# Expert slots by rank, an earlier routing order and moved operands in a two-block transformer kernel

## The chip, the cores and the metric

The kernel runs on one core of one Trainium2 chip. The metric is the device time of one execution in microseconds (us). Five engines run their own instruction streams: TensorE (PE; its weight loads are listed as PEld), VectorE (DVE), ScalarE (ACT), GpSimd (POOL) and SyncE (SP), which here issues nearly all DMAs.

## The reference

256 tokens of width 1024 pass through two blocks. The first has two layers, each a mixer (attention with pooling in layer 0, gating with convolution in layer 1) and a mixture of experts (MoE). The second has two layers of attention branches and an MLP. The change is mostly in the MoE of the first block:

```python
g_prob = softmax(t @ rg_w + rg_b); g_p, g_idx = top_k(g_prob, 1)            # 4 groups
e_sel = e_logits[group g_idx]                                               # 4 experts of the group
top_p, top_i = top_k(softmax(e_sel), 2); top_p = top_p / sum(top_p)
weights = g_p * top_p; expert_id = g_idx * 4 + top_i                        # 2 of 16 experts per token
for wg, wu, wd, cw in experts:
    acc = acc + ((silu(t @ wg) * (t @ wu)) @ wd) * cw[:, None]
```

So 512 assignments of tokens to 16 experts are computed in each layer, and how many tokens an expert has is known only on the chip.

## The kernel before

**The MoE.** `moe` computes router logits (lg) and from them the chosen experts (selb); products with triangular and all-ones matrices (rank, L490 to L494) give each token its place among the tokens of its expert (rk) and each expert its count (cn). One-hot matrices (oh; weighted ow) are built from the places by `slots`; `gather` multiplies the normed tokens, as high and low parts whi and wlo, with oh into the slots of a group of experts (gps, L543, evicted as xg or ug); `up` makes the gate and up products (gu, L566), `turn` transposes and weights (htp, L580), `down` makes the down product (yp, L600) and scatters back to tokens (y, L609) with ow transposed. A slot group has 256 columns: four experts of 64 slots (CAP), and `prepare(q)` builds group q.

**The steps.** STEPS has seven steps. Experts 0 to 3 are fixed and fill steps one and two, so their weights are loaded ahead (`chunk`). The other twelve are sorted by their counts: `key`, `more`, `perm`, `order`, and as integers `ints` (L642 to L658). SyncE reads these (TENSOR_LOAD, L725) before it issues the load of an expert's weights (`dyn`, L730). Step five holds four experts of 32 slots as four column tiles of TensorE, the others two experts of 64 slots as two tiles of 64 columns. Up, gather and down of neighbouring steps are interleaved on TensorE.

**Overflow.** `more_blocks` counts what doesn't fit. In the last round the engines read `over` and `rest` (L725) and branch (L788): if any expert has more than its slots, `overflow` runs gather, up, turn and down once more for the two largest, whose weights were kept (step LAST), and under L791 and L793 further blocks for other experts.

**Order and queues.** Each engine runs its stream in the order of the built program, which a scheduler makes from the code; `keep_in_program_order` pins an instruction. Between router and gather TensorE has products for the conditioning (mps<-w,cpad, L382), which `cond` spreads over the program. Weights come in 1 MB chunks through rings of 13 slots; SyncE issues them in order and waits when no slot is free.

**Products in three parts.** `mm3` (L168 to L170) makes each fp32 product of 256 columns as three: weights whi with moving high part, whi with low part, wlo with high part. `split` (L140, L141) makes whi and wlo from a chunk on ScalarE and VectorE. `tm` (L201 to L203) does the same with 512 columns. The MLP up products are fm<-oTh, its down products d<-hidh; the attention projections are fm<-acth, those of the mixers fm<-ah.

**Start.** `warm(22)` issues bf16 products on zeros at the start of the program; the first mixer's tm products follow the first conditioning round (`cond.finish()`).

Of the kernel before, what the change touches and what calls it, by code (L numbers as in the profile page):

```python
# [49 lines left out]
NC1 = _lay(C1T, [("stri", 128), ("cos2d", 128), ("sin2d", 128), ("slot", 64), ("first", 4), ("rank", 12), ("gap", 38), ("less", 16)])  # L50
# [9 lines left out]
STEPS = ((0, 1), (2, 3), (4, 5), (6, 7), (8, 9, 10, 11), (12, 13), (14, 15))  # L60
PART = ((0, 0), (0, 1), (1, 0), (1, 1), (2, 0), (3, 0), (3, 1))
LAST = 6
RANKS = (2, 3, 4, 5, 8, 9, 10, 11, 6, 7, 1, 0)
# [4 lines left out]
def build(tc, I, O):  # L68
# [3 lines left out]
    with es:  # L72
# [3 lines left out]
        psum = es.enter_context(tc.tile_pool(name="psum", bufs=1, space=PSUM))  # L76

# [32 lines left out]
        ring_b = b1.enter_context(tc.tile_pool(name="ring_b", bufs=7))  # L110
        pb = c1.tile([128, NPB], F32, name="pb")
# [7 lines left out]
        epst = const.tile([128, 16], F32, name="epst")[:, 0:1]  # L119
# [308 lines left out]
        def moe(layer, norm, rc, work, blocks):  # L428
# [29 lines left out]
            def b4(x):  # L458
                return x.to_broadcast([128, 2, 4, 4])

            red(em, le, ALU.max)
            red(gm, gl, ALU.max)
            V.tensor_tensor(e2, le, b4(em), op=ALU.subtract)
            A.activation(e2, e2, AF.Exp)
            V.tensor_tensor(ge, gl, bc(gm, 4), op=ALU.subtract)
            A.activation(ge, ge, AF.Exp)
            V.tensor_tensor(oe, gl, bc(gm, 4), op=ALU.is_equal)
            V.tensor_tensor(oe, oe, FG, op=ALU.mult)
            red(es_, e2, ALU.add)
            red(om, oe, ALU.max)  # L470
            V.reciprocal(es_, es_)
            V.tensor_tensor(og, oe, bc(om, 4), op=ALU.is_equal)
            V.tensor_tensor(pr, e2, b4(es_), op=ALU.mult)
            red(gs, ge, ALU.add)
            V.reciprocal(gp, gs)

            p8 = pr.rearrange("p b g j -> p (b g) j")
            other, own = (p8.unsqueeze(i).to_broadcast([128, 8, 4, 4]) for i in (2, 3))
            V.tensor_tensor(eq, other, own, op=ALU.is_equal)
            V.tensor_tensor(gt, other, own, op=ALU.is_gt)  # L480
            V.tensor_tensor(eq, eq, C("less").rearrange("p (i j) -> p i j", i=4).unsqueeze(1)
                            .to_broadcast([128, 8, 4, 4]), op=ALU.mult)
            V.tensor_tensor(gt, gt, eq, op=ALU.add)
# [13 lines left out]
            V.tensor_tensor(sel, pr.rearrange("p b g j -> p b (g j)"), selb, op=ALU.mult)  # L497
            red(om, sel, ALU.add)
            V.reciprocal(om, om)
            V.tensor_tensor(om, om, gp, op=ALU.mult)  # L500
            V.tensor_tensor(cw, sel, bc(om, 16), op=ALU.mult)

# [5 lines left out]

            rk = t(16, "rk")
# [4 lines left out]
            def slots(n, ranks, weights, cap=CAP):  # L514

                shape = [128, n, CAP]
                oh = small.tile([128, 2, n, CAP], F32R, name="oh", tag=f"oh{n}", bufs=2 if n == 4 else 1)
                ow = small.tile([128, 2 * n * CAP], F32, name="ow", tag=f"ow{n}", bufs=2 if n == 4 else 1)
                ow = ow[:, 0:2 * n * cap].rearrange("p (b n s) -> p b n s", b=2, n=n)
                for b in range(2):  # L520
                    V.tensor_tensor(oh[:, b], C("slot").unsqueeze(1).to_broadcast(shape),
                                    ranks[:, b].unsqueeze(2).to_broadcast(shape), op=ALU.is_equal)
                    V.tensor_tensor(ow[:, b], oh[:, b, :, 0:cap].bitcast(F32),
                                    weights[:, b].unsqueeze(2).to_broadcast([128, n, cap]), op=ALU.mult)
                return oh, ow
# [3 lines left out]
            def gather(oh, n):  # L529

                w = n * CAP
                flip[0] ^= n == 4
                if flip[0] or n < 4:
                    xg = small.tile([128, NK, w], F32, name="xg", tag="xg")
                else:
                    xg = c1.tile([128, NK, w], F32, name="ug", tag="ug")
                per = 512 // w
                for q in range(NK // per):
                    gp_ = (ops if q % 2 else acc)("gps")
                    for m, (part, b) in enumerate((p_, b_) for p_ in (ah, al) for b_ in range(2)):  # L540
                        for i in range(per):
                            k = per * q + i
                            T.matmul(gp_[:, w * i:w * i + w], part[b][:, 128 * k:128 * k + 128],  # L543
                                     oh[:, b].rearrange("p e s -> p (e s)"),
                                     start=(m == 0 and i == 0), stop=(m == 3), skip_group_check=True)
# [10 lines left out]
            def up(x_, s0, gus, between=lambda: None, n=2):  # L556

                each = 128 // n
                gu = acc("gu")
                for h in range(2):  # L560
                    if h:
                        between()
                    w = [gus(h, e) for e in range(n)]
                    for k in range(4):
                        for e in range(n):
                            T.matmul(gu[each * e:each * e + each, :],  # L566
                                     x_[:, 4 * h + k, s0 + CAP * e:s0 + CAP * e + each],
                                     w[e][:, 512 * k:512 * k + 512],
                                     start=(h == 0 and k == 0), stop=(h == 1 and k == 3),
                                     tile_position=(0, each * e))  # L570
# [20 lines left out]
            def down(turned, dns, first, last, n=2):  # L591
                ht, back, cws = turned
                each = 128 // n
                wd = [dns(e) for e in range(n)]
                yg = pair([128, D], "yg", small, bufs=2)
                for q in range(2):
                    yp = (ops if q else acc)("yp")
                    for k in range(2):
                        for e in range(n):
                            T.matmul(yp[each * e:each * e + each, :],  # L600
                                     ht[:, 128 * k + each * e:128 * k + each * e + each],
                                     wd[e][:, 1024 * k + 512 * q:1024 * k + 512 * q + 512],
                                     start=(k == 0), stop=(k == 1), tile_position=(0, each * e))
# [11 lines left out]
            g2 = const.tile([128, NK], F32, name=f"g2_{layer}")  # L615
# [5 lines left out]

            def prepare(q):
                oh, ow = slots(4, (rkp if q else rk)[:, :, 4 * q:4 * q + 4], (cwp if q else cw)[:, :, 4 * q:4 * q + 4],
                               CAP // 2 if q == 2 else CAP)
                if q == 0:
# [7 lines left out]
                quarter[q] = gather(oh, 4), ow  # L633
# [4 lines left out]

            iota = C("slot")[:, 0:16]
            order, key, more_ = (small.tile([128, 16], F32, name=n, tag=n) for n in ("order", "key", "more"))  # L640
            few = small.tile([128, 24], F32, name="few", tag="few")[:, 0:16]
            V.scalar_tensor_tensor(key, cn, 16.0, iota, op0=ALU.mult, op1=ALU.add)  # L642
            in2 = small.tile([128, 12, 16], F32, name="in2", tag="in2")
            perm = small.tile([128, 12, 16], F32, name="perm", tag="perm")
            G.memset(perm, 0.0)
            G.memset(more_, 0.0)
            shape = [128, 12, 12]
            V.tensor_tensor(in2[:, :, 0:12], key[:, 4:16].unsqueeze(1).to_broadcast(shape),
                            key[:, 4:16].unsqueeze(2).to_broadcast(shape), op=ALU.is_gt)
            V.tensor_reduce(more_[:, 4:16], in2[:, :, 0:12], axis=AX.X, op=ALU.add)  # L650
            V.tensor_tensor(perm[:, :, 4:16], more_[:, 4:16].unsqueeze(1).to_broadcast(shape),
                            C("rank").unsqueeze(2).to_broadcast(shape), op=ALU.is_equal)
            shape = [128, 12, 16]
            V.tensor_tensor(in2, perm, iota.unsqueeze(1).to_broadcast(shape), op=ALU.mult)
            V.tensor_reduce(order[:, 4:16], in2, axis=AX.X, op=ALU.add)
            ints = small.tile([128, 16], I32, name="ints", tag="ints")
            intr = small.tile([128, 10], I32, name="intr", tag="intr")
            V.tensor_copy(ints[:, 4:16], order[:, 4:16])  # L658

            rkp, cwp = t(16, "rkp"), t(16, "cwp")  # L660
            for dst_, src_ in ((rkp, rk), (cwp, cw)):
                for b in range(2):
                    V.tensor_tensor(in2, perm, src_[:, b].unsqueeze(1).to_broadcast(shape), op=ALU.mult)
                    V.tensor_reduce(dst_[:, b, 4:16], in2, axis=AX.X, op=ALU.add)
# [3 lines left out]
            def more_blocks():  # L668
# [3 lines left out]
                ov, ov2, cnt, last = (small.tile([128, 16], F32, name=n, tag=n) for n in ("ov", "ov2", "cnt", "last2"))  # L672
                rest = small.tile([128, 2], F32, name="rest", tag="rest")
# [3 lines left out]
                V.scalar_tensor_tensor(key, few, CAP / 2, cn, op0=ALU.mult, op1=ALU.add)  # L677
# [1196 lines left out]
```

## Time and profile before

| what | value |
|---|---|
| median of 3 runs | 1494.14 us (1490.57 to 1494.27) |
| the profiled execution | 1494.22 us, span 1492.5 us |
| mean granted TensorE clock | 0.985 |
| busy: PE, DVE, ACT, POOL | 1453.1, 851.7, 654.1, 27.3 us |
| HBM read | 322 MB, 216 GB/s over the span |

How to read it: the first block runs to about 600 us (the MoE of layer 0 from about 172 to 334, of layer 1 from about 458 to 594), the second block after it in two similar halves. Idle time of an engine matters only where TensorE waits for that engine. A clock of 1.00 in a stretch is 2.4 GHz, 0.5 is 1.2 GHz. Matmuls are pipelined, so the time from the start of one to the start of the next is what a product costs, not its own listed duration.

### The profile page before, as it was taken

The page shows a single profiled execution, that of the slowest core. Times are in us where ns is not written, and L with a number is a line of the kernel's source. Part 1 is how long each engine was busy: PE and PEld are TensorE (multiplying, and loading weights), DVE is VectorE, ACT ScalarE, POOL GpSimd, SP SyncE. Part 2 cuts the span into 40 slices and gives each one's busy share as a digit, 9 for nine tenths or more (in the row PEclk, how much of TensorE's full clock was granted, in tenths as well). Part 3 has the DMA queues.
Part 4 walks back from the last instruction along what each step waited for, and adds up shares of the span by engine and source line. Part 5 has one row for each costly group of instructions (what it writes and reads, how often), then busy time and mean ns, then how long its engine had stood idle before and what let it go on. Part 6 is the DMA issues. An engine that isn't in the chain of part 4 may idle for free.

```text
span 1492.5 us, 25477 instructions
## 1 busy us (share of the span) xinstructions
PE 1453.1 (97%) x10370; PEld 1168.0 (78%) x10372; DVE 851.7 (57%) x1666; ACT 654.1 (44%) x1108; POOL 27.3 (2%) x63
## 2 busy tenths in 40 slices
PE   8999899989999998999999999999999999999998
PEld 3756644446985443798789999999898799999998
DVE  2765452126637222758776765556759767755554
ACT  2544311124433111565664554444565654644443
POOL 0000000000000000010000000000100000000000
PEclk9999999999999999999999999999999999999999
DMA  9964799949484986644125555553443234555540
GB/s 394 400 283 171 296 372 366 398 167 374 173 335 191 404 360 238 211 158 171 58 90 193 191 205 183 185 197 143 155 167 144 69 131 170 188 208 198 177 162 29
DMA packets 47006, 324.85 MB, mean 218 GB/s; under 512 B 5601, under 2 KB 5985, under 8 KB 8481
## 3 DMA queue, kind: packets, MB, share of 16 engines
q1 hardware_dynamic: 45360, 320.12, 56.3%
q8 instruction: 86, 1.41, 0.4%
q10 hardware_dynamic: 1296, 1.55, 0.3%
q0 software_dynamic: 224, 1.46, 0.3%
q14 instruction: 40, 0.32, 0.1%
HBM read 322.06 MB, written 1.05 MB: 216 GB/s over the span
## 4 chain that ended last, share of the span: by engine, by line
PE 57%; DVE 2%; ACT 1%; issue 0%; DVEq 0%; ACTq 0%
PE fm L169 10%; PE fm L170 10%; PE fm L168 10%; PE d L169 4%; PE d L168 4%; PE d L170 4%; PE sp L1504 1%; PE tm L201 1%; PE tm L202 1%; PE tm L203 1%; PE lf L169 1%; PE lf L170 1%; PE lf L168 1%; PE po L1493 1%; PE ptp L1487 1%; DVE wlo L141 1%
## 5 line engine op out<-in xcount | busy, mean ns | idle before, releaser
L141 DVE TENSOR_TENSOR wlo<-w,whi 128x1024 fp32r<-128x1024 f32 (+1 forms) x314 | 378.4, 1208 | 254.1 <-ACT whi L140 252.9
L140 ACT CAST whi<-w 128x1024 fp32r<-128x1024 f32 (+1 forms) x314 | 324.3, 1035 | 388.2 <-PE fm L169 234.7
L168 PE MATMUL fm<-acth,whi 128*128 128x256 f32 x592 | 169.4, 286 | 0.0
L169 PE MATMUL fm<-actl,whi 128*128 128x256 f32 x592 | 168.2, 284 | 0.0
L170 PE MATMUL fm<-acth,wlo 128*128 128x256 f32 x592 | 167.9, 284 | 0.0
L170 PE MATMUL d<-hidh,wlo 128*128 128x256 f32 x512 | 144.1, 282 | 0.0
L169 PE MATMUL d<-hidl,whi 128*128 128x256 f32 x512 | 144.0, 281 | 0.0
L168 PE MATMUL d<-hidh,whi 128*128 128x256 f32 x512 | 143.9, 281 | 0.0
L169 PE MATMUL fm<-oTl,whi 128*128 128x256 f32 x512 | 143.6, 281 | 0.0
L170 PE MATMUL fm<-oTh,wlo 128*128 128x256 f32 x512 | 143.3, 280 | 0.0
L168 PE MATMUL fm<-oTh,whi 128*128 128x256 f32 x512 | 143.1, 280 | 0.0
L169 PEld LDWEIGHTS fm<-actl,whi 128*128 128x128 f32 x592 | 112.5, 190 | 2.3 <-issue 2.3
L168 PEld LDWEIGHTS fm<-acth,whi 128*128 128x128 f32 x592 | 113.1, 191 | 1.0 <-issue 0.8
L170 PEld LDWEIGHTS fm<-acth,wlo 128*128 128x128 f32 x592 | 112.4, 190 | 1.3 <-issue 1.0
L169 PEld LDWEIGHTS fm<-oTl,whi 128*128 128x128 f32 x512 | 96.8, 189 | 0.4 <-DVE oTl L1118 0.4
L169 PEld LDWEIGHTS d<-hidl,whi 128*128 128x128 f32 x512 | 96.7, 189 | 0.4 <-DVE hidl L141 0.4
L168 PEld LDWEIGHTS fm<-oTh,whi 128*128 128x128 f32 x512 | 96.9, 190 | 0.0
L168 PEld LDWEIGHTS d<-hidh,whi 128*128 128x128 f32 x512 | 96.8, 189 | 0.1
L170 PEld LDWEIGHTS d<-hidh,wlo 128*128 128x128 f32 x512 | 96.8, 189 | 0.1
L170 PEld LDWEIGHTS fm<-oTh,wlo 128*128 128x128 f32 x512 | 96.8, 189 | 0.0
L600 PE MATMUL yp<-w,ht 128*64 128x512 f32 (+1 forms) x272 | 71.8, 622 | 6.6 <-PEq L791 3.2
L566 PE MATMUL gu<-w,ug 128*64 128x512 f32 x256 | 62.2, 598 | 0.0
(537 smaller groups left out, 2875.1 us busy)
## 6 DMA issues: line engine op xcount, KB each, us to landing
w<-gu SPq DMA_DIRECT2D x64, 1024.0 KB, 8.7
w<-mod SPq DMA_DIRECT2D x48, 1024.0 KB, 10.7
w<-dn SPq DMA_DIRECT2D x32, 1024.0 KB, 10.0
w<-gw SPq DMA_DIRECT2D x32, 1024.0 KB, 4.8
w<-up SPq DMA_DIRECT2D x32, 1024.0 KB, 4.7
w<-dw SPq DMA_DIRECT2D x32, 1024.0 KB, 4.7
w<-tm SPq DMA_DIRECT2D x12, 1024.0 KB, 4.9
w<-oin SPq DMA_DIRECT2D x8, 1024.0 KB, 8.8
```

Of the source, the lines that this page charges most:

```text
L140: A.copy(hi, src)
L141: V.tensor_sub(lo, src, hi.bitcast(F32))
L168: T.matmul(out, ws[0], xs[0], start=first, stop=False, skip_group_check=skip)
L169: T.matmul(out, ws[0], xs[1], start=False, stop=False, skip_group_check=skip)
L170: T.matmul(out, ws[1], xs[0], start=False, stop=last, skip_group_check=skip)
L201: T.matmul(ps, at[0], ww[0], start=first, stop=False, skip_group_check=True)
L202: T.matmul(ps, at[1], ww[0], start=False, stop=False, skip_group_check=True)
L203: T.matmul(ps, at[0], ww[1], start=False, stop=k == NK - 1, skip_group_check=True)
L566: T.matmul(gu[each * e:each * e + each, :], x_[:, 4 * h + k, s0 + CAP * e:s0 + CAP * e + each], w[e][:, 512 * k:512 * k + 512], start=(h = ...
L600: T.matmul(yp[each * e:each * e + each, :], ht[:, 128 * k + each * e:128 * k + each * e + each], wd[e][:, 1024 * k + 512 * q:1024 * k + 51 ...
L1487: T.transpose(tp[:, 128 * c:128 * c + 128], prs[g][:, 128 * c:128 * c + 128], ident)
L1493: T.matmul(po[64 * g:64 * g + 64, 0:S], vals(g, 0), prs[g][:, 0:S], start=first, stop=False, tile_position=(0, 64 * g), skip_group_check=True)
```

## The change

Slots: the two experts with the most tokens get 96 slots, the next six 64, the last six 32, still in seven steps of 128 slots. Experts 0 and 1 alone are fixed and fill step one; fourteen are sorted. An expert of 96 slots and one of 32 share a step as four column tiles, three of them on the same weights (steps six and seven). GROUPS lists the groups: the first gather is 128 wide, the others 256. Overflow has one kind of block, read through one integer, and the last step's weights are no longer kept for it.

Order: the sort (`order`, `ints`) stands in `prepare(0)` right behind the first one-hots; ranking uses the shifted logits e1, and the softmax weights are computed later, in `weights()`. `prepare` for the next groups is called after steps one, two and four (before: one, three and five).

Start: `warm(11, True)` adds eleven pinned products behind the first `cond.finish()`.

Operands: `apart` allocates empty tiles (16, 24, 23, 16, 48 and 48 columns) in several pools; epst, few, m8, dv and vss are smaller or share a buffer; gap is 48 wide. They compute nothing.

```diff
-STEPS = ((0, 1), (2, 3), (4, 5), (6, 7), (8, 9, 10, 11), (12, 13), (14, 15))
-RANKS = (2, 3, 4, 5, 8, 9, 10, 11, 6, 7, 1, 0)
+RANKS = (2, 3, 4, 5, 6, 7, 8, 9, 10, 11, 0, 1, 12, 13)
+GROUPS = (((0, 2, 64),), ((2, 4, 64),), ((6, 2, 64), (8, 4, 32)), ((12, 2, 96), (14, 2, 32)))
+STEPS = ((0, 0, ((0, 64), (1, 64))), (1, 0, ((2, 64), (3, 64))), (1, 128, ((4, 64), (5, 64))),
+         (2, 0, ((6, 64), (7, 64))), (2, 128, ((8, 32), (9, 32), (10, 32), (11, 32))),
+         (3, 0, ((12, 32), (12, 32), (12, 32), (14, 32))), (3, 128, ((13, 32), (13, 32), (13, 32), (15, 32))))
+PREPARE = {0: 1, 1: 2, 3: 3}
...
+        def apart(pool, n):
+            V.memset(pool.tile([128, n], F32, name=f"gap{n}", tag=f"gap{n}"), 0.0)
...
-        def warm(n):
+        def warm(n, here=False):
...
-                T.matmul(ps, zero[:, 0:128], zero, start=True, stop=True)
+                ins = T.matmul(ps, zero[:, 0:128], zero, start=True, stop=True)
+                if here:
+                    tc.keep_in_program_order(ins)
...
+            V.tensor_tensor(e1, le, b4(em), op=ALU.subtract)
             V.tensor_tensor(oe, gl, bc(gm, 4), op=ALU.is_equal)
+            A.activation(e2, e1, AF.Exp)
+            p8 = e1.rearrange("p b g j -> p (b g) j")
...
+            def weights():
+                V.tensor_tensor(ge, gl, bc(gm, 4), op=ALU.subtract)
+                A.activation(ge, ge, AF.Exp)
+                red(es_, e2, ALU.add)
...
+                V.tensor_tensor(cw, sel, bc(om, 16), op=ALU.mult)
...
-            for k in range(4):
-                for e in range(n):
-                    T.matmul(gu[each * e:each * e + each, :],
+                    for k in range(4):
+                        for i, (p_, n) in enumerate(tiles):
+                            T.matmul(gu[n * i:n * i + n, :], x_[:, 4 * h + k, s0 + n * i:s0 + n * i + n],
+                                     w[p_][:, 512 * k:512 * k + 512],
...
+            def sort():
+                V.scalar_tensor_tensor(key, cn, 16.0, iota, op0=ALU.mult, op1=ALU.add)
...
+                V.tensor_copy(ints[:, 2:16], order[:, 2:16])
...
-                    over, rest = (value(intr, i, (EN.PE, EN.Activation, EN.DVE, EN.Pool), 8) for i in range(2))
+                    over = value(intr, 0, (EN.PE, EN.Activation, EN.DVE, EN.Pool), 8)
                     with tc.If(over > 0):
-                        overflow(res, cwp[:, :, 14:16], lambda h, e: weights_of(LAST, h, e),
-                                 lambda e: weights_of(LAST, 2, e))
-                        with tc.If(rest > 0):
-                            overflow_any(0)
+                        overflow_any(0)
+                        with tc.If(over > 2):
...
             cond.finish()
+            warm(11, True)
...
-                    m8 = at.tile([128, 8], F32, name="m8", tag="m8", bufs=2)
+                    m8 = at.tile([128, 8], F32, name="m8", tag="m8")
...
+            E["apart"](at, 48)
...
+            E["apart"](ml, 48)
...
-                    V.memset(ml.tile([128, 32], F32, name="gap", tag="gap"), 0.0)
+                    V.memset(ml.tile([128, 48], F32, name="gap", tag="gap"), 0.0)
```

The order of instructions at three places, before and after. TensorE at the start of the MoE of layer 0 (mps: conditioning products; rank: the counting products), before:

```order
L242 MATMUL nps<-cst,sqs 128x1 x2
L382 MATMUL mps<-w,cpad 32x512 x31
L490 LDWEIGHTS strib
L490 MATMUL rank<-selb,strib 128x16
L491 LDWEIGHTS strib
L491 MATMUL rank<-selb,strib 128x16
```

and after, with the first gather behind it:

```order
L498 MATMUL rank<-selb,strib 128x16
L499 LDWEIGHTS strib
L499 MATMUL rank<-selb,strib 128x16
L500 LDWEIGHTS onesb
L500 MATMUL rank<-selb,onesb 128x16
L501 LDWEIGHTS onesb
L501 MATMUL rank<-selb,onesb 128x16
L502 LDWEIGHTS onesb
L502 MATMUL rank<-selb,onesb 128x16
L395 MATMUL mps<-w,cpad 32x512 x24
L566 MATMUL gps<-oh,whi 128x128 x8
```

Of the 32 conditioning products that stood ahead of the rank products, 24 now stand behind them, and the gather follows.

VectorE from the ranks on in layer 0 (rk: ranks; oh, ow: one-hots; key, in, more, perm, order, ints: the sort), before:

```order
L511 TENSOR_TENSOR rk<-off_1561,rank 128x32
L512 COPY cn<-rank 128x16
L521 TENSOR_TENSOR oh<-cst_80,rk 128x256 x2
L523 TENSOR_TENSOR ow<-oh,cw 128x256 x2
L627 SCALAR_TENSOR_TENSOR late<-rk,rc 128x2
L642 SCALAR_TENSOR_TENSOR key<-cn,cst_80 128x16
L631 SCALAR_TENSOR_TENSOR wlo<-ut,late,whi 128x512 x4
L551 TENSOR_SCALAR xg<-gps,mod_114 128x256
L648 TENSOR_TENSOR in_1656<-key 128x12x12
```

and after, from the sort's first large step to its integers:

```order
L654 TENSOR_TENSOR in_1601<-key 128x14x14
L681 SCALAR_TENSOR_TENSOR wlo<-ut,late,whi 128x512
L656 TENSOR_REDUCE more<-in_1601 128x14
L681 SCALAR_TENSOR_TENSOR wlo<-ut,late,whi 128x512
L657 TENSOR_TENSOR perm<-more,cst_82 128x14x14
L681 SCALAR_TENSOR_TENSOR wlo<-ut,late,whi 128x512
L660 TENSOR_TENSOR in_1601<-perm,cst_82 128x224
L681 SCALAR_TENSOR_TENSOR wlo<-ut,late,whi 128x512
L661 TENSOR_REDUCE order<-in_1601 128x14
L450 TENSOR_REDUCE gs<-ge 128x2
L522 RECIPROCAL om<-om 128x2
L662 CAST ints<-order 128x14
```

The sort is now between the low parts and ahead of the first eviction xg, which stands 28 rows below the last row shown; before, the first eviction stood ahead of the sort.

SyncE around the first read of the integers in layer 0 (gu: gate and up weights, dn: down weights), before:

```order
L136 DMA w<-gu 128x2048 x4
L136 DMA w<-mod 128x2048
L136 DMA w<-gu 128x2048 x4
L136 DMA w<-dn 128x2048 x2
L725 TENSOR_LOAD ints
```

and after:

```order
L147 DMA w<-gu 128x2048 x3
L147 DMA w<-mod 128x2048
L147 DMA w<-gu 128x2048
L752 TENSOR_LOAD ints
L752 ISA x2
```

Ten chunks of fixed experts' weights stood ahead of the first read, now four do.

## Rows read from the trace of the kernel before

**Rows 1.** The page, first part: busy us (share of the span) xinstructions.

```profile
PE 1453.1 (97%) x10370; PEld 1168.0 (78%) x10372; DVE 851.7 (57%) x1666; ACT 654.1 (44%) x1108; POOL 27.3 (2%) x63
```

**Rows 2.** Stretches of TensorE: us, busy (x), clock, DMA share, GB/s.

```profile
307.20:329.58 22.38, 17.44 (x100) 0.99 0.19 77
586.45:589.32 2.87, 0.00 (x1) 0.89 0.03 9
```

**Rows 3.** Waits of TensorE, 300:335 and 575:600: us in total, times, longest.

```profile
PE yp L600 <- PEq L791: 3.2, 1, 3.2
...
PE yp L600 <- PEq L788: 2.9, 1, 2.9
```

**Rows 4.** Stretches with six quads and with seven pairs of column tiles.

```profile
257.00:259.58 2.58, 2.58 (x25) 1.00 0.90 378
192.53:195.53 3.00, 3.00 (x15) 1.00 0.72 218
```

**Rows 5.** The tile selb in layer 0: ns min/median/max, first and last start, forms, waits.

```profile
L487 DVE SCALAR_TENSOR_TENSOR selb<-before,og x1: 191/191/191, 175.6 to 175.6; 128x32 bf16<-128x32 f32 x1
...
L490 PE MATMUL rank<-selb,strib x1: 182/182/182, 182.3 to 182.3; 128*128 128x16 bf16 x1
...
  DVE rk L511: 5.7, 1
```

**Rows 6.** Waits of TensorE, 170:215.

```profile
PE gps L543 <- DVE wlo L631: 0.8, 2, 0.7
PE gps L543 <- DVE oh L521: 0.8, 1, 0.8
```

**Rows 7.** A stretch of TensorE in the first gather of layer 0.

```profile
185.26:189.53 4.27, 4.11 (x16) 0.60 0.94 397
```

**Rows 8.** Waits of TensorE, 455:495.

```profile
PE rank L490 <- DVE selb L487: 1.7, 1, 1.7
PE gps L543 <- DVE om L500: 1.0, 1, 1.0
PE gps L543 <- DVE wlo L631: 0.2, 1, 0.2
```

**Rows 9.** Waits of SyncE's queue, 160:300 and 455:580, and GB/s in fortieths of 455:600.

```profile
SPq L725 <- DVE ints L658: 10.9, 1, 10.9
...
SPq L730 <- PE gu L566: 49.1, 14, 9.6
...
SPq L725 <- DVE ints L658: 13.3, 1, 13.3
...
GB/s 140 149 0 0 142 325 405 427 423 423 434 429 418 427 425 429 260 395 380 398 377 414 314 142 420 418 427 429 226 292 364 427 432 423 350 9 7 5 59 411
```

**Rows 10.** The start: waits of TensorE in 15:45, then stretches.

```profile
PE tm L201 <- ACT whi L140: 2.9, 1, 2.9
...
31.16:34.03 2.87, 0.00 (x0) 0.70 1.00 421
34.03:39.24 5.21, 5.21 (x12) 0.51 1.04 430
39.24:45.00 5.76, 5.76 (x27) 1.00 1.01 427
```

**Rows 11.** Stretches in the attention projections, 24 product starts each.

```profile
780.25:783.13 2.88, 2.88 (x27) 1.00 0.17 23
783.13:785.95 2.82, 2.82 (x26) 1.00 0.83 349
785.95:788.83 2.88, 2.88 (x26) 1.00 0.78 225
```

**Rows 12.** Stretches in the MLP, 48, 23 and 48 product starts.

```profile
933.29:938.74 5.45, 5.45 (x50) 1.00 0.47 165
944.34:947.05 2.71, 2.71 (x25) 1.00 0.38 157
950.03:955.74 5.71, 5.71 (x50) 1.00 0.52 192
```

More of the change, by code (lines that the diff above doesn't have):

```diff
@@ L49 @@
 C1T = {}
-NC1 = _lay(C1T, [("stri", 128), ("cos2d", 128), ("sin2d", 128), ("slot", 64), ("first", 4), ("rank", 12), ("gap", 38), ("less", 16)])
+NC1 = _lay(C1T, [("stri", 128), ("cos2d", 128), ("sin2d", 128), ("slot", 96), ("first", 4), ("rank", 14), ("gap", 4), ("less", 16)])
 NCB = 128 + 128 + 30 + 512
@@ L554, in moe, with up @@
             ys = [sps("y0"), sps("y1"), sps("y2"), tps("y3")]
-            def up(x_, s0, gus, between=lambda: None, n=2):
-                each = 128 // n
+            def up(x_, s0, gus, between=lambda: None, tiles=((0, 64), (1, 64))):
                 gu = acc("gu")
@@ L589, in turn, with down @@
                 return ht, back, cws
-            def down(turned, dns, first, last, n=2):
+            def down(turned, dns, first, last, tiles=((0, 64), (1, 64))):
                 ht, back, cws = turned
-                each = 128 // n
-                wd = [dns(e) for e in range(n)]
+                wd = {p_: dns(p_) for p_ in dict.fromkeys(p_ for p_, _ in tiles)}
                 yg = pair([128, D], "yg", small, bufs=2)
@@ L598, in down @@
                     for k in range(2):
[L599 to L603, printed above, removed]
+                        for i, (p_, n) in enumerate(tiles):
+                            T.matmul(yp[n * i:n * i + n, :], ht[:, 128 * k + n * i:128 * k + n * i + n],
+                                     wd[p_][:, 1024 * k + 512 * q:1024 * k + 512 * q + 512],
+                                     start=(k == 0), stop=(k == 1), tile_position=(0, n * i))
                     hi, lo = pick(yg, lambda z: z[:, 512 * q:512 * q + 512])
@@ L613, in down @@
                 return yg[0]
-            g2 = const.tile([128, NK], F32, name=f"g2_{layer}")
+            g2 = const.tile([128, NK], F32, name="g2", tag="g2")
             def collect(m):
@@ L632, in prepare @@
                                                    ah[b][:, cols].bitcast(F32), op0=ALU.mult, op1=ALU.subtract)
-                quarter[q] = gather(oh, 4), ow
+                    weights()
+                at = 0
+                for p0, n, w in GROUPS[q]:
+                    weighted(ow, oh, at, w, cws__[:, :, p0:p0 + n])
+                    at += n * w if w < 96 else w
+                quarter[q] = gather(oh, 256 if q else 128), ow
             prepare(0)
             cond.keep()
[L639 to L658, printed above, removed]
+            shape = [128, 14, 16]
             rkp, cwp = t(16, "rkp"), t(16, "cwp")
@@ L733, in overflow @@
             def overflow(ranks, weights, gus, dns):
-                oh, ow = slots(2, ranks, weights)
-                xo = gather(oh, 2)
-                hh = up(xo, 0, gus)
-                down(turn(hh, lambda b: ow[:, b].rearrange("p e s -> p (e s)"), "o"), dns, False, False)
+                oh = small.tile([128, 2, 128], F32R, name="oh", tag="oh2")
+                ow = small.tile([128, 2, 128], F32, name="ow", tag="ow2")
+                plain(oh, 0, CAP, ranks)
+                weighted(ow, oh, 0, CAP, weights)
+                hh = up(gather(oh, 128, True), 0, gus)
+                down(turn(hh, lambda b: ow[:, b], "o"), dns, False, False)
             def overflow_any(i):
```

192 lines of the change are left out of this document (99 added, 93 removed).

## The prediction

> **What bounds the kernel now.** I read the page's busy times first: TensorE is busy for 1453.1 us of a span of 1492.5 us [rows 1], so there are 39 us of idle in all, and whatever is taken away must be work, slow work or an idle of TensorE. I therefore looked for four things with the stretches: a block of work that need not run, idle in front of the MoE, half-clock stretches, and the spacing of the 256-column products that fill most of the program. VectorE and ScalarE count only where TensorE waits for them by name. The profiled execution took 1494.22 us, as good as the median of 1494.14, so a saving read in it is taken from 1494.2.
>
> **Part 1, the overflow block.** From the reference's own inputs and routing I counted the tokens per expert: in layer 0 two experts have 77 and 76, no other above 52; in layer 1 the largest have 61 and 44. With 64 slots layer 0 runs the overflow block for its two largest, layer 1 runs none. In the trace this is the stretch from 307.20, where the block's gather starts, to 329.58, where the last step's down product starts: 22.38 us. Layer 1 shows what stays when the block is skipped: 2.87 us between the last scatter and the same down product [rows 2], the idle that the list of waits puts on the sequencer at the branch (3.2 us in layer 0, 2.9 in layer 1) [rows 3]. With 96 slots both layers skip it: 22.4 - 2.9 = **19.5 us** off, all TensorE's own time. What pays for the slots: the two big experts are packed with a small one each, as four tiles of 32 columns, three of which read the same weights, where a step had two tiles of 64. In before a quad of 32-column tiles from four experts starts every 0.43 us (six quads in 2.58 us) and a pair of 64-column tiles also every 0.43 us (seven pairs in 3.00 us) [rows 4]. So the packing costs nothing by these rows, if tiles that share weights run side by side as others do.
>
> **Part 2, the order comes early.** In layer 0 the rank product that VectorE waits for stands behind 32 products on the conditioning weights; its input selb is there at 175.6, it starts at 182.3 and VectorE idles 5.7 us for it [rows 5]. After, it stands behind 8 of them, so the ranks, the first one-hots, the low parts (wlo) and the sort run under the other 24 (175.3 to 182.3). What of this is on the path: the gather's waits of 0.8 and 0.8 us [rows 6], about 1 us between the rank product and the first gather, and the slow gather at 185.26 to 189.53, where the granted clock was 0.60 [rows 7]: some 1.5 us over full speed. That is 4 us. Against it stands a new wait: by the order the first eviction of the gather (xg) is queued on VectorE behind some 30 small operations of sort, weights and overflow bookkeeping; at 0.17 to 0.35 us each I get the first xg at about 188, TensorE idle about 2 us for it, partly in place of waits that I counted. The ends are 0 (the new wait eats all, and a half-clock stretch follows it) and 4; I take **3 us**, nearer the upper end because the first half of the sort runs under the products. In layer 1 TensorE waits 1.7 us for selb, 1.0 us for the end of the softmax chain (om) and 0.2 for wlo [rows 8]. The chain is cut to what ranking needs (no reciprocals, ranking on the shifted logits, weights later): selb about 1 us earlier, the om wait gone, and the 0.2 to 1 us seams inside the gather shorter, because its parts stand in one piece. Ends 1 and 4; I take **3 us**.
>
> The sort's result also frees SyncE, which waits 10.9 us in layer 0 and 13.3 in layer 1 for the integers [rows 9]. They come about 9 and 3 us earlier, but only 4 weight chunks stand ahead of them where 8 and 2 did. From there 44 chunks of 1 MB follow; at the 427 GB/s of the full stretches [rows 9] one takes 2.45 us, and the last of layer 1 lands near 577, used near 586; the tightest, the down chunks of the sixth step, have about 2 us to spare by my count. SyncE's long waits (49.1 us for slots that TensorE still reads [rows 9]) say that the stream has slack between. I book nothing.
>
> **Part 3, eleven more warm-up products** fill the 2.9 us in which TensorE waits for the first whi; after that idle the granted clock was 0.51, the lower of its two levels (1.2 of 2.4 GHz), for 5.21 us, then 1.00 [rows 10]. At full clock the twelve products in that stretch would take about half, so the prize is up to 2.6 us; if the warm-up itself runs slow, it lasts beyond the idle and costs up to 2 us. I take **1.9 us** gained, since the clock before the idle was full and the warm-up keeps the engine busy through it.
>
> **Part 4, the operands moved.** The empty tiles (apart, gap) and the smaller buffers compute nothing; they shift addresses. I took the addresses that the two built programs give their tiles and, for each 256-column product, the moving operand's byte address less that of the next weights, modulo 128. Before, some 3,450 of the 6,480 such products of the projections and the MLPs have remainder 0, most others 64; after, nearly all have 64. In the attention's projections stretches of 24 products alternate between the two: with 0 they take 2.88 us (120.0 ns each), with 64 2.82 us (117.7) [rows 11], while the DMA share of these same stretches goes from 0.17 to 0.83 in no step with it. In the MLP 48 products with 0 take 5.71 us (119.0), 48 with 64 take 5.45 (113.6), and 23 others with 64 take 2.71 (117.7) [rows 12]. So the two go apart wherever I look, by 2.3 ns (attention) and 1.3 to 5.4 ns (MLP, mean 3.3). With remainder 0 stand 1,680 products in the attentions and the two mixers, which I price like the first, and 1,770 in the MLPs and the projection ahead of them: 1,680 x 2.3 = 3.9, 1,770 x 3.3 = 5.8, together **9.7 us**; the ends are 6 and 13. The 512-column products of the mixers (some 330 with remainder 0) show no difference that I can tell, and get nothing. The shorter buffers (m8, dv) make nothing wait that TensorE waits for: it idles nowhere in the MLPs.
>
> The Trainium skill speaks against this part: TensorE: Matmul & The Clock Gate, section Back-to-back issue gap, gives the warm gap of an isolated product as columns over 2.4 GHz plus 2.5 ns, some 109 ns for 256 columns, with no term for addresses. By that rule the move gives nothing; the rows above, with 113.6 to 120.0 ns for one shape at one clock, do not agree with one price.
>
> **Sum.** 19.5 + 3 + 3 + 1.9 + 9.7 = 37.1; 1494.2 - 37.1 = **1457**.
>
> **Rivals.**
> First, the addresses are not the cause: the two spacings go with something that changes along with the chunks, such as which half of the stage buffers is being written. For it: within remainder 64 there are two spacings, 113.6 and 117.7, that the addresses don't explain. Against: three kinds of stages agree. Part 4 falls away: 1494.2 - 27.4 = 1467. The rule of the skill named above leads here too.
> Second, the early order is spent: the first eviction comes so late that TensorE's new idle is followed by another half-clock stretch in both layers, or the weights of layer 1's last steps come late by 2 or 3 us. Parts 2 then give 0 to 2 instead of 6: 1461 to 1463.
> Third, slower: the three tiles that share one expert's weights do not run side by side, since all three would stream the same addresses at once, which no row of before shows. If they run one after another, a quad takes three times 0.43 us, 0.86 more. Steps five and six have 16 quads up and 4 down each, 80 in both layers: 69 us, and the time is 1457 + 69 = 1526. It turns the sign from 0.46 us more per quad, about a doubling. Against it: the pairs and quads of before all start side by side.
> Fourth, the capacity doesn't do what it says, as layer 0 still takes the branch: 19.5 less, 1476. The counts speak against it.
>
> **How the numbers follow.** Forecast 0.62; addresses 0.18; early order spent 0.14; tiles that share 0.04; branch 0.02. The time is that of the likeliest, 1457. The range takes in the low end of the unknowns (part 4 at 13, part 2 at 8, some 1451) and the high end of the first rival: 1450 to 1468. A measurement of this kernel tells 0.3%, 4.5 us, from no change; all cases but the third lie well beyond it on the fast side: faster 0.95, same 0.01, slower 0.04.
>
> **What would show it.** In the profile after: no gather of 128 columns between the last scatter of step six and the last down product of layer 0, and an idle of about 2.9 us there, at the branch; rank in layer 0 near 176, ints near 181; the first up step ending some 3 us earlier against the start of the MoE in both layers; the first mixer's products at full clock from their start; spacings of 120 ns gone from the attention and the MLP, and 24 products in 2.72 to 2.83 us. I am wrong if the fifth and sixth steps take visibly longer than the others, or if the spacing stays at 119 to 120 ns with the new addresses.

## The result and the profile after

The changed kernel took 1449.32 us (median of 4, 1442.21 to 1451.32), before 1494.12: a ratio of 0.970 (95% interval 0.967 to 0.973), 45 us less. The forecast was 1457, the range 1450 to 1468: the direction was right, the time lies just below the range, and the sum of 37 us was 8 too small. Measured once more, with the last experiments, the same kernel took 1445.69 beside 1493.18 for the kernel before. The profiled execution took 1449.81 us with a span of 1448.1. The page's busy times:

```profile
PE 1410.9 (97%) x10473; PEld 1133.6 (78%) x10475; DVE 846.1 (58%) x1664; ACT 650.4 (45%) x1101; POOL 28.8 (2%) x63
```

TensorE is as full as before [rows 1], so the whole gain is in its own time. To see where, cut the program where the second block's attention products begin. The stretches from the start to that cut and from there to the last matmul (us, busy (xinstructions), clock, DMA share, GB/s), before:

```profile
0.00:636.11 636.11, 605.94 (x3513) 0.97 0.75 301
636.11:1485.86 849.75, 846.87 (x6860) 1.00 0.44 156
```

and after:

```profile
0.00:610.40 610.40, 584.21 (x3615) 0.97 0.77 314
610.40:1441.45 831.05, 826.43 (x6860) 1.00 0.45 159
```

The second block runs the same 6,860 matmuls at the same clock and is 18.7 us shorter. Nothing but addresses and the sizes and counts of a few small buffers changed there. The first block, with the routing, the overflow and the warm-up, gave 25.7.

Where the prediction expected an idle of 2.9 us at the branch [rows 2], the waits of TensorE after show 5.4 us in layer 0 and 3.3 in layer 1, and the stretches show the idle and then the last down products at the low clock (first layer 0, then layer 1):

```profile
PE yp L618 <- PEq L815: 5.4, 1, 5.4
...
PE yp L618 <- PEq L815: 3.3, 1, 3.3
```

```profile
296.90:302.18 5.28, 0.01 (x1) 0.85 1.01 419
302.18:307.84 5.66, 5.66 (x31) 0.54 0.95 356
558.23:561.84 3.61, 0.28 (x4) 0.74 0.03 7
561.84:567.41 5.57, 5.57 (x32) 0.56 0.02 3
```

The start of the MoE, from the first gather product to the first up product and from there to the end of the second up, before (layer 0, then layer 1):

```profile
183.41:189.53 6.12, 5.28 (x24) 0.72 0.96 407
189.53:211.46 21.93, 21.78 (x109) 1.00 0.84 339
462.53:467.77 5.24, 5.09 (x25) 0.69 0.00 0
467.77:489.70 21.93, 21.78 (x108) 1.00 0.83 325
```

and after:

```profile
180.23:184.70 4.47, 3.79 (x36) 1.00 0.86 297
184.70:203.24 18.54, 18.36 (x100) 1.00 1.01 415
432.62:440.33 7.71, 6.72 (x32) 0.57 0.14 29
440.33:461.84 21.51, 21.33 (x101) 0.92 1.01 423
```

Layer 0 gains 5.0 us here (28.05 to 23.01), layer 1 loses 2.1 (27.17 to 29.22): its gather takes 7.71 us at a clock of 0.57, where that of layer 0 takes 4.47 at 1.00.

### The profile page after: what moved, and what is told of

Read it like the earlier page. It is cut to its first block, busy times and chain, and to the rows that moved or that the text cites. A ratio compares the mean times of both kernels' runs of the same rounds, so it can differ in the third digit from the quotient of the medians.

```text
span 1448.1 us, 25693 instructions
## 1 busy us (share of the span) xinstructions
PE 1410.9 (97%) x10473; PEld 1133.6 (78%) x10475; DVE 846.1 (58%) x1664; ACT 650.4 (45%) x1101; POOL 28.8 (2%) x63
## 4 chain that ended last, share of the span: by engine, by line
PE 56%; DVE 3%; ACT 1%; issue 1%; DVEq 0%; ACTq 0%
PE fm L180 9%; PE fm L179 9%; PE fm L181 9%; PE d L180 4%; PE d L179 4%; PE d L181 4%; PE tm L213 1%; PE tm L214 1%; PE sp L1529 1%; PE tm L212 1%; DVE wlo L152 1%; PE po L1518 1%; PE ptp L1512 1%; PE lf L181 1%; PE lf L180 1%; PE lf L179 1%
## 5 line engine op out<-in xcount | busy, mean ns | idle before, releaser
L181 PE MATMUL fm<-acth,wlo 128*128 128x256 f32 x592 | 165.0, 279 | 0.7 <-DVE wlo L152 0.7
L618 PE MATMUL yp<-w,ht 128*32 128x512 f32 (+1 forms) x320 | 72.6, 666 | 8.7 <-PEq L815 8.7
L587 PE MATMUL gu<-w,ug 128*32 128x512 f32 (+1 forms) x384 | 60.7, 596 | 0.0
```

The lines of the kernel that those rows point to most:

```text
L181: T.matmul(out, ws[1], xs[0], start=False, stop=last, skip_group_check=skip)
L587: T.matmul(gu[n * i:n * i + n, :], x_[:, 4 * h + k, s0 + n * i:s0 + n * i + n], w[p_][:, 512 * k:512 * k + 512], start=(h == 0 and k == 0) ...
L618: T.matmul(yp[n * i:n * i + n, :], ht[:, 128 * k + n * i:128 * k + n * i + n], wd[p_][:, 1024 * k + 512 * q:1024 * k + 512 * q + 512], sta ...
```

## The experiments

Numbers without a fence in this section and the next come from the starts of single matmuls in the trace of the run named. "Spacing" is the time from the start of one 256-column product to that of the next, averaged over those that follow each other directly (105 to 126 ns).

**Undoing the operand moves.** Edit to the changed kernel (and the old sizes of epst, m8, dv, vss and gap):

```diff
-            V.memset(pool.tile([128, n], F32, name=f"gap{n}", tag=f"gap{n}"), 0.0)
+            return
```

> The changed kernel with its operand moves undone: no empty tiles, the old buffer counts and sizes. By the built addresses the products have the remainders of before again (some 3,450 at 0). The changed kernel took 1449.3 us. Theory A, as in the prediction: each product pays for its own remainder, 9.7 us in all: 1459. Theory B, formed on the two traces: a stretch with remainder 0 (119 to 120 ns) also leaves the products after it at 117.8 ns, and without any nearly all run at 113.3; the mean of the 256-column products fell from 118.2 to 114.6 ns, which on 6,480 is 23 us: 1468 to 1472. Theory C, the addresses do nothing: 1449.

Measured: 1466.57 us (0.982 of before, 0.981 to 0.984), 17 us over the changed kernel as first measured and 21 over its second measurement. Its two stretches, cut as above:

```profile
0.00:610.66 610.66, 584.53 (x3617) 0.97 0.78 314
610.66:1459.50 848.84, 845.59 (x6860) 1.00 0.44 156
```

The first block is that of the changed kernel, the second that of the kernel before, to 1 us. So the addresses are worth some 18 us in the second block and little in the first. How little, the two first blocks don't say to 1 us, since each has low-clock stretches of its own; by the spacing, the 576 mixer products fm<-ah there went from 119.9 to 117.4 ns, some 1.4 us. Theory A (9.7 us) and theory C (nothing) both fall; B's size was right for the products, and the time lies 1.4 us below its range.

**The moves alone, in the kernel before.** The same tiles and sizes in the second block only:

```diff
+        E["apart"](wk, 16)
...
+            E["apart"](at, 48)
...
+            E["apart"](ml, 48)
...
-                    V.memset(ml.tile([128, 32], F32, name="gap", tag="gap"), 0.0)
+                    V.memset(ml.tile([128, 48], F32, name="gap", tag="gap"), 0.0)
```

> The kernel before with the operand moves of the second block alone (empty tiles, buffer counts and sizes there; the first block's mixers keep remainder 0). By the undo in e1 these addresses are worth 17.8 us from the first attention product to the end. If they act alone, without the other parts: 17 to 18 us under the kernel before, near 1476. By the term of the prediction (each product for itself): 8 us under it, 1486.

Measured: 1476.94 us (0.989 of before, 0.987 to 0.991), 16 us less by the medians. Its second block takes 830.05 us, as in the changed kernel:

```profile
637.45:1467.50 830.05, 825.13 (x6859) 1.00 0.45 159
```

The effect needs none of the other parts. The 16 us have an interval of 14 to 20, which takes in the 17 to 18 expected and leaves out the 8 of the prediction's term.

**One tile of the MLP moved.** The hidden tile of the MLP lies 64 bytes further in the first of two runs, 32 bytes further in the second (8 in place of 16):

```diff
-                hid[cj] = pair([128, 2, S], "hid", ml, bufs=2)
+                hid[cj] = [z[:, 16:16 + 2 * S].rearrange("p (k s) -> p k s", k=2)
+                           for z in pair([128, 2 * S + 32], "hid", ml, bufs=2)]
```

> The changed kernel with one address moved: the hidden tile of the MLP lies 64 bytes further, so the 1,536 MLP down products (d<-hid) have remainder 0, and all others, the MLP up products (fm<-oT, 1,536) among them, keep 64 and their addresses. Theory A (each product pays for its own): down products at 119 to 120 ns, up products at 113.3 as in the changed kernel: 1,536 x 6.3 = 9.7 us, 1459. Theory B (a stretch with 0 leaves its state to the next): up products at 117.8 too, another 1,536 x 4.5 = 6.9 us: 1466. Theory C: 1449.

> The changed kernel with the MLP's hidden tile 32 bytes further: its 1,536 down products have remainder 96. With 0 there they took 119.1 ns and the kernel 6.8 us more. If only remainder 0 is slow: 113 to 114 ns and the time of the changed kernel. If anything but 64 is slow: 116 ns or more (the 192 products of the kernel before with remainder 32 took 116.8), 3 to 7 us more.

Measured: 1456.09 us (0.976 of before, 0.974 to 0.977) and 1456.14 us (0.976, 0.974 to 0.978); the changed kernel took 1449.32 and 1445.69 in its two measurements, the second on the chip of the run with 32 bytes. So the tile moved by 64 bytes costs 7 to 10 us, where theory A asked for 9.7 and theory B for 16.6; moved by 32 bytes it costs 10 us on the same chip, where 3 to 7 were expected. The groups of MLP products by line (busy us, mean ns of one) show the down products slower, and the up products, whose addresses did not move against their weights, slower too, by a third to two thirds as much. Changed kernel:

```profile
L181 PE MATMUL d<-hidh,wlo 128*128 128x256 f32 x512 | 142.0, 277 | 0.0
...
L179 PE MATMUL fm<-oTh,whi 128*128 128x256 f32 x512 | 141.2, 277 | 0.0
```

Remainder 0:

```profile
L181 PE MATMUL d<-hidh,wlo 128*128 128x256 f32 x512 | 145.0, 283 | 0.0
...
L179 PE MATMUL fm<-oTh,whi 128*128 128x256 f32 x512 | 142.3, 279 | 0.0
```

Remainder 96:

```profile
L181 PE MATMUL d<-hidh,wlo 128*128 128x256 f32 x512 | 144.2, 282 | 0.0
...
L179 PE MATMUL fm<-oTh,whi 128*128 128x256 f32 x512 | 142.6, 279 | 0.0
```

The spacings say it more sharply, for the MLP's two kinds and for all products:

| kernel | down: remainder, ns | up: remainder, ns | all, ns |
|---|---|---|---|
| before | 0: 119.1; 64: 116.2 | 0: 119.5; 64: 116.3 | 118.2 |
| changed | 64: 114.0 | 64: 113.9 | 114.5 |
| moves undone | 0: 119.1; 64: 116.2 | 0: 119.5; 64: 116.3 | 118.2 |
| hidden tile at 0 | 0: 119.1 | 64: 115.8 | 116.2 |
| hidden tile at 96 | 96: 119.0 | 64: 116.8 | 116.5 |

Two things follow. Remainder 96 is as slow as 0, so it isn't that 0 alone collides; of the remainders tried in the MLP, 64 is the fast one. By the addresses of the kernel before it is the difference that tells, and not the place of either operand: with the moving operand and the next weights both at 0, or both at 64, modulo 128 its products took 119 to 120 ns on average, with one at 0 and the other at 64, either way round, 115.7 to 117.4. And 64 has two spacings, some 113.3 and 117.8 ns, between which one and the same pair of addresses changes. In the changed kernel the up products whose weights lie at one address (24 product starts each) do so within 33 us:

```profile
856.64:859.47 2.83, 2.83 (x27) 1.00 0.00 0
889.71:892.43 2.72, 2.72 (x27) 1.00 0.44 184
```

Once at 113.3 the stream stays there: in the changed kernel's first MLP from 868 us on nearly every stretch does, up and down alike. With a slow tile between them, 46% (remainder 0) and 23% (96) of the up products' spacings are below 115.5 ns, against 87%. So a stretch with a bad remainder costs its own products 5 ns each and often takes the fast spacing from the next ones: theory A has the down products right (119.1), and the up products, at 115.8 and 116.8, lie between the 113.3 of A and the 117.8 of B. What switches a stream from 117.8 to 113.3 stays open. It is not settled by the remainder, as the mixers of the first block show: their products fm<-ah went from 119.9 (0) to 117.4 ns (64), and the 192 products fm<-mixh took 119.9 with 0 (in the run with the moves of the second block alone), 116.8 with 32 (before) and 117.8 with 64 (after), so there 64 is no better than 32.

**Without the warm-up.**

```diff
-            warm(11, True)
```

> The changed kernel without the eleven warm-up products. As predicted: the first mixer's products start after an idle of about 2.9 us and run 5 to 7 us at the lower clock, and the mixer's first 256-column products come 1.9 us later: 1451. If the warm-up only moves the low clock into itself: 1449.

Measured: 1446.20 us (0.970 of before, 0.968 to 0.971), between the two measurements of the changed kernel. In the trace the mixer's first 256-column products come at 126.7 us, in the changed kernel and seven runs that share its start between 125.4 and 125.9: about 1 us is what the warm-up gives by the traces, and the times don't show it. (In the run with the moves undone the clock was at 0.55 already ahead of the warm-up, and those products come at 128.0.) In the profiled execution of the changed kernel the warm-up itself ran at the low clock and overran the idle (the warm-up, then the tm products):

```profile
31.16:34.88 3.72, 3.72 (x12) 0.58 0.99 412
34.88:40.00 5.12, 5.12 (x24) 1.00 1.03 433
```

Without it (the idle, then the tm products):

```profile
31.16:34.02 2.86, 0.00 (x0) 0.52 0.99 417
34.02:39.14 5.12, 5.12 (x14) 0.60 1.04 431
```

But in the seven other runs the warm-up ran at 1.00 and ended 0.5 us before the tm products, which ran at 1.00 too. The changed kernel in its second measurement (the warm-up, then the tm products):

```profile
31.09:33.63 2.54, 2.54 (x13) 1.00 1.03 433
34.12:39.24 5.12, 4.80 (x20) 1.00 1.04 430
```

There the first twelve tm products take 3.5 us, without the warm-up 4.8 and in the kernel before 5.2. The full clock doesn't halve them: in the same trace TensorE waits 0.5 us for whi and 0.3 for wlo around them. So the lead is 1.2 us after twelve products, and about 1 us of it is left at the first 256-column products.

**Without the branch.** The lines from `over = value(...)` to the end of the overflow blocks are gone.

> The changed kernel without the branch and the overflow blocks (they are not run with these inputs, so only inputs with more tokens per expert would come out wrong). The changed kernel idles 5.4 us and 3.3 us at the branch and then runs the last down products at a clock of 0.54 and 0.56. If only the idle is at stake: 8 us less, 1441. If the low clock goes with it (the last down products take 5.7 and 5.6 us in place of about 3.5): 12 us less, 1437.

Measured: 1435.71 us (0.962 of before, 0.960 to 0.964), 10 to 14 us under the changed kernel. The stretches around the same place in layer 0:

```profile
299.61:299.81 0.20, 0.20 (x3) 1.00 1.06 451
299.81:303.40 3.59, 3.59 (x33) 1.00 1.00 420
```

The last down product follows after 0.20 us, and its 32 parts take 3.6 us at a clock of 1.00 in place of 5.7 at 0.54. So a branch that is not taken costs some 7.5 us in layer 0 and 3 to 6 in layer 1: the idle, and the low clock that mostly follows it (in layer 1, from the first start to the last, the last down products took 3.2 us in four of the twelve traces with the branch, at a clock of 1.00, and 4.4 to 6.0 in the others). The kernel needs the branch for other inputs.

**The overflow block alone, in the kernel before.**

```diff
-                    with tc.If(over > 0):
+                    with tc.If(over > 6):
```

> The kernel before with the overflow branch kept but never taken (the condition asks for more than six overflowing blocks; 25 assignments of layer 0 beyond 64 slots are left out). The prediction's step: 22.4 us gone, 2.9 us of idle in their place: 19.5 us under the kernel before, 1474. If a skipped branch costs in layer 0 what the changed kernel shows there (idle 5.4 us, then the down products at the low clock): 16 to 17 us under it, 1477.

Measured: 1476.05 us (0.989 of before, 0.987 to 0.991), 17 us less (interval 13 to 20). The skipped branch of layer 0 and the down products behind it:

```profile
307.84:313.39 5.55, 0.28 (x3) 0.82 0.81 337
313.39:319.37 5.98, 5.98 (x16) 0.59 0.90 322
```

By the waits 5.3 us of the first stretch are idle, as in the changed kernel (5.4), so the idle belongs to the place and not to the changed kernel. In all runs that skip the branch it is 5.3 to 6.3 us in layer 0, where weights stream in (DMA share 0.70 to 1.01), and 2.8 to 3.3 in layer 1, where they hardly do (0.00 to 0.12). The kernel before skips the inner branch of its overflow block at that place of layer 0 without a stream (0.02) and idles 3.2 us. That the stream makes the idle longer fits all of these; it was not tried by itself.

**The sort, late in both layers and late in layer 1 alone.** In the first run `sort()` stands behind `prepare(0)`; in the second only in layer 1:

```diff
-                    sort()
+                    if not layer:
+                        sort()
...
             cond.keep()
+            if layer:
+                sort()
```

> The changed kernel with the sort behind the first gather again; ranks and weights stay. If the early sort matters through SyncE's loads: the integers come some 4 us later, the chunks behind them too, and layer 1 with its tight stream loses 2 to 4 us, 1451 to 1453. If it stands in the way of the first eviction on VectorE: the first up product of layer 0 comes 1 to 2 us earlier, and the time falls by as much, 1447. If neither: within 1 us.

> The changed kernel as it is, beside the next two on the same chip: 1445 to 1450, the ground for what differs by little.

> The changed kernel with the sort early in layer 0 alone and behind the first gather in layer 1. With the sort late in both layers, layer 1 went 2.3 us faster from the gather to the end of the second up, and layer 0's steps behind it 1.4 us slower. If both come from where the sort stands (in layer 1 no conditioning products follow the rank products, so VectorE's sort holds up the low parts that TensorE waits for; in layer 0 24 of them cover it): 1 to 2 us under the changed kernel, the gather of layer 1 in 6.4 us in place of 7.7, layer 0 as in the changed kernel. If they were luck of the clock: the same time.

Measured: late in both 1445.19 us (0.968 of before, 0.966 to 0.970); the changed kernel again 1445.69 (0.968, 0.966 to 0.971); late in layer 1 alone 1443.77 (0.967, 0.965 to 0.968). By the times the three are not told apart, but the stages agree over the traces. In layer 1 the gather takes 7.7 us in seven runs with the early sort, and 6.4 and 6.1 with the late one (here the last run, from the gather to the first up product and on to the end of the second up):

```profile
429.02:435.16 6.14, 5.48 (x32) 0.79 0.00 0
435.16:455.99 20.83, 20.65 (x101) 0.90 0.92 367
```

In layer 0, whose 24 conditioning products cover the sort, moving it behind the gather costs 1.4 us in the later steps (94.7 us against 93.3 from the end of the second up to the branch), and leaving it early keeps that (93.4). The first up product of layer 0 comes no earlier with the late sort (4.4 us behind the first gather product, 4.0 to 4.6 with the early one), so there the sort stands in the way of no eviction that counts.

**Filling the idle before the gather.**

```diff
+            warm(5 if layer else 13, True)
             rp = tps("rank")
...
+            if layer:
+                warm(4, True)
```

> The changed kernel with warm-up products on zeros in TensorE's idle around the rank products (13 ahead of them in layer 0; 5 ahead and 4 behind in layer 1). In the changed kernel TensorE ran the gather and the first up of layer 1 at 0.57 and 0.78 of its clock after that idle (7.4 and 8.3 us, against 3.5 and 6.5 in layer 0). If the idle causes the low clock: 4 to 6 us less in layer 1 and 1 to 2 in layer 0, 1443. If the low clock comes anyway: no gain, or the warm-up's own time lost, 1449 to 1451.

Measured: 1450.55 us (0.971 of before, 0.969 to 0.973), no gain. It doesn't answer the question: in the trace the warm-up products do not stand at the idle. In layer 0 they run at 180.2 to 182.8 us, behind the conditioning products, and hold the gather up by 2.6 us; in layer 1 behind the first half of the gather. Whether a filled idle would keep the clock up there stays open.

## Why the prediction was off, point by point

- **Part 4, the operands: right in kind, half in size, and this is the step that failed.** 9.7 us were booked, with ends of 6 and 13; the second block alone gave 18.7, the undo 17 to 21, the moves alone 16. The count (3,450 products with remainder 0) held by the addresses of the built programs. What was wrong is the price and whom it falls on. I read the difference between neighbouring stretches, 120.0 and 117.7 ns [rows 11], as the whole difference. But the 117.7 is not what remainder 64 costs when no stretch with 0 is near: the same row group of the MLP had 113.5 in one place [rows 12], and I averaged that in as one of two equal cases. With all at 64 some three quarters of the products run there, those too that already had 64. The mean over all 6,480 fell by 3.7 ns, some 24 us of spacing, of which the second block's stretches show 17.8 to 19.7. The first rival (addresses not the cause, 0.18) is refuted by the undo, the moves alone and the one tile moved, which changes no buffer's use. The rule of the Trainium skill that I weighed (TensorE: Matmul & The Clock Gate, Back-to-back issue gap) has one price for this shape, by its formula for an isolated product at the warm clock an estimated 109 ns for 256 columns. The traces don't agree with one price: they have four levels at a clock of 1.00, 113.3, 117.8, 119 and 120 ns, and the lowest is 4 ns above it.
- **Part 1, the overflow: 19.5 booked, 17 measured (13 to 20).** The block's 22.4 us went. The step that took layer 1's 2.9 us as the cost of skipping was too cheap for layer 0, which idles 5.3 us there. The low clock behind the idle adds less than 1 us (the last down products take 5.5 us from first start to last, with the block 4.6 at a clock of 0.66). The counts were right, so the fourth rival falls.
- **Part 2, layer 0: 3 booked, about 8 measured.** The new wait in front of the first up is there but short (0.96 us between the last gather product and the first up product, where I had 2). The slow gather is gone: its clock is 1.00, before it was 0.60 [rows 7]. From gather to second up 5.0 us; the gather starts some 1 to 2 us earlier; and the steps behind the second up take 93.3 us where the kernel before without overflow takes 95.3. I had booked nothing for that; that gather and up alternate less often would explain it, but was not tried by itself.
- **Part 2, layer 1: 3 booked, nothing measured.** The rank products came 1.2 us and the first gather product 1.4 us earlier against the mixer's last product, as expected; the gather then lost it. I had read layer 1 like layer 0, though no conditioning products follow its rank products. The sort therefore stands, on VectorE, between the one-hots and the low parts, and TensorE waits 1.0 us for wlo and 0.7 for oh, where it had waited 0.2 for wlo and 1.0 for om [rows 8]; the low clock in the second half of the gather makes it longer. In the first half the clock does not set the time: all seven traces with the early sort have 7.7 us from the first gather product to the first up product, at clocks from 0.57 to 0.75, as a faster first half waits longer for wlo (1.2 us at the longest in the second trace of the changed kernel, 0.8 in the first). The list of waits of TensorE, 425 to 462 us, after:

```profile
PE gps L566 <- DVE wlo L681: 1.0, 2, 0.8
PE gps L566 <- DVE oh L535: 0.7, 1, 0.7
PE rank L498 <- DVE selb L495: 0.5, 1, 0.5
```

  The second rival has its mechanism here, in one layer and at another place than I put it.
- **Part 3, the warm-up: 1.9 booked, about 1 measured by the traces.** The mechanism came as booked in seven of the nine traces that have it: the warm-up ran at 1.00 through the idle, and the tm products behind it at 1.00. In the profiled execution of the changed kernel it ran at 0.58 and overran the idle by 0.9 us, the other case that I had priced. What was too large is the prize: at full clock the first twelve tm products take 3.5 us and not half of 5.2.
- **The third rival** (tiles that share weights) did not come, and I had priced it with 4 quads of the down product a step where the trace has 32 parts, so 8: the 64 parts of the seventh step's up run in the time of the 32 parts before. After, then before:

```profile
281.35:287.83 6.48, 6.48 (x65) 1.00 1.01 427
```

```profile
291.64:298.13 6.49, 6.49 (x32) 1.00 1.02 427
```

- **The weights of layer 1** came in time: TensorE waits for no weight chunk of the MoE in the list of waits of the whole run.

Together: 18.7 for the second block, 17 for the overflow, 8 for layer 0's order (the mixer's shorter spacing ahead of it included) and 1 for the warm-up make 44.7 of 44.8 us. That it closes so well is in part luck. By the starts of single matmuls the first block gains 1.4 us up to the mixer's first 256-column product, 1.8 from there to the gather of layer 0, 5.0 to the end of the second up and 17.0 to the last scatter of layer 0; then 4.4 in the mixer of layer 1, where the profiled execution of the kernel before had two low-clock stretches and that of the changed kernel one; and it loses 1.8 from the rank products of layer 1 to the end of its second up and 2.1 from there to the second block. The last three cancel. With 18.7 in place of 9.7 and the other terms as booked the sum would have been 46: their errors (-2.5, +5, -3, -1) nearly cancel too, so it is part 4 that made the sum too small.

## What to carry to other kernels

When one kind of product has several spacings at one clock, look at how moving and stationary operands lie towards each other in memory before looking for waits, and take the best spacing seen anywhere as the upper end of what the fix can give, and the step between neighbours as the lower: a slow stretch can take its neighbours with it. A move that pays in one layer because other work covers it must be read again in every other layer for that cover. A branch not taken has a price of its own, and it is to be read at its own place, with the clock that follows it.

## What was not expected of the hardware

Of TensorE's 256-column products with the moving operand's address less that of the next weights at 64 modulo 128 bytes, most run every 113.3 ns; at 0 and at 96 they run every 119 to 120 on average. At 64 there is a second spacing of 117.8 ns that stays over many products, with no address changed. A branch that is not taken stopped TensorE for 2.8 to 3.3 us with little DMA traffic and for 5.3 to 6.3 us under a weight stream. The clock over the products behind it was 0.54 to 0.66 in layer 0, and in layer 1 0.50 to 0.69 in eight traces and 1.00 in four. One and the same stretch of the first block (the last products of the second mixer, fm<-mixh) ran with a low clock in three traces, those of the kernel before, the changed kernel and the undo, and without in the others, which moved the time by 1 to 3 us; that is why a difference of a few us is read here from the stages and not from the medians alone.
